# In-projection duals of a hybrid conv block: PSUM pairs that turn, wide additions, q split after DRAM

## The chip, the cores and the metric

The kernel runs on one core of one Trainium2 chip. The metric is the device time of one execution in microseconds; before the change it is 1518.36 us (median of three runs, 1518.31 to 1518.46). A core has TensorE (PE, matmuls into PSUM), VectorE (DVE), ScalarE (ACT), GpSimd (POOL) and SyncE (SP, which here only issues DMAs). PSUM has eight banks of 128 partitions by 512 fp32 words.

## What is computed

One trunk layer on x of 1024 tokens by 1024 channels, float32:

```python
h = rms_norm(x, norm_mix_g) * (1 + sc1) + sh1
b_s, c_s, v_s, v_c, gl_c, gate_br = split(h @ w_in)      # 7 blocks of 1024 columns
y_a = (b_s * causal_dwconv3(c_s * v_s)) @ w_short_out    # the factor before w_short_out is "q"
u   = causal_dwconv31(v_c * sigmoid(gl_c)) + conv_conf_b
y_b = silu(layer_norm(u)) @ w_conf_out
g_a, g_b = split(sigmoid(gate_br))
x = x + g1 * ((g_a * y_a + g_b * y_b) @ w_o)
h2 = rms_norm(x, norm_ffn_g) * (1 + sc2) + sh2
a, b = split(h2 @ w_ffn_in)
x = x + g2 * ((silu(a) * b) @ w_ffn_out)
out = rms_norm(x, final_norm_g)
```

## The kernel before, in words

Activations lie transposed: channels on partitions, tokens along the free dimension, in two halves of 512. Each float32 operand is split into a high and a low part (`th`/`tl` for activations, `wh`/`wl` for weights) and each product is three matmuls (`mm3`, L285, L286, L288). `split_w` makes `wh` on ACT (L207) and `wl` on DVE or, in the in-projection, on POOL (L208).

Most of the in-projection runs in twelve **duals**. A dual works on a pair of entries of `PAIRS`, which are four column blocks of 128, two for each half-index p, as 2 by 2 block matrices multiplied with seven products instead of eight. `PRODUCTS = "1265734"` is their order. The weight sums (`dual_units`, L230 to L234) and the low halves are POOL's. Each product is 2 (p) x 4 (k) x 3 matmuls of 128x512, 24 in all, accumulated in one of three banks per p: x takes products 1, 6, 7 and 4 on top of each other, y takes 2, z takes 5 and 3. A weight set is prepared two products ahead (`AHEAD`), and the plan of weights is fetched by `next_w`.

After each half product, `evac` in `win_evac` (L569) takes the bank's state out: products 1 and 6 are copied by ACT to SBUF (L579), 5 too (L594); 2, 3 and 7 are added by DVE to what lies there (`plus`, L547); 4 goes to its use from PSUM. From these come the four blocks C11, C12, C21, C22 of each entry. Four kinds of entry follow: "u" (the conv's input, v times sigmoid of gl), "p" (c times v, then the 3-tap `short_conv`, L538 and L540, into `sc`), "q" (b times `sc`, L551 and L589), "g" (sigmoid, then a store of the gate to DRAM by ACT's queue, L616). `q_store` (L527) splits q into high and low in a `qs` tile, ACT cast (L531) and POOL subtraction (L532), and stores both by SP (L534). `q_load` (L621) brings the split halves back to operand tiles of the `t` pool by SP, four after each product of the last dual.

Beside the duals DVE runs the 31-tap conv, `conv(j)` for eight channel blocks: 46 taps each (L649) on two PSUM banks of `ps2`, with ACT at its beginning (L653) and end (L662); `add_conv` sums the result on POOL (L669). A tap's place in DVE's order is bounded by `tc.issue_after`: tap n of block j comes after a certain one of the `plus` instructions, listed in `reads`, so that all are spread over the first 66 of the 72. Otherwise the order on each engine is set by a planner that goes by program order as priority and by its own estimate of times; on the chip each engine then runs its instructions in that order. Tiles come from pools with a fixed number of buffers: `uc` (8 of 128x1054) for u, p, sc, sig, qs and cv; `gs` (6 of 128x512) for small results; `ps` (6 single PSUM banks) and `ps2` (2).

After the duals comes `ya`: for each of eight column blocks, q (all eight channel blocks) times `w_short_out`, then the layer norm, `yb`, `mix`, and the FFN.

Of the kernel before, what the change touches and what calls it, by code (L numbers as in the profile page):

```python
# [34 lines left out]
F32 = mybir.dt.float32  # L35
# [4 lines left out]
P = 128  # L40
# [43 lines left out]
CONV_READS = 66  # L84

# [24 lines left out]
def block_kernel(ctx: ExitStack, tc: tile.TileContext, x0, xT, c, vecs, ada, w_first, w_plain, w_duals,  # L110
# [21 lines left out]
    psp = pool("ps", 6, space=bass.MemoryType.PSUM)  # L132
    ps2p = pool("ps2", 2, space=bass.MemoryType.PSUM)
    dram = pool("scratch", 1, space=bass.MemoryType.DRAM)
    gsp = pool("gs", 6)
# [3 lines left out]

    def ps_tile(name):  # L140
        return psp.tile([P, H], F32, tag="ps", name=name)
# [10 lines left out]
    def g_tile(name):  # L152
        return gsp.tile([P, H], F32, tag="gs", name=name)
# [373 lines left out]
    def q_store(j):  # L527

        for h in range(2):
            s = uc_tile("qs", T, F32R)  # L530
            nc.scalar.copy(s[:, :H], sc[j][:, halves[h]])  # L531
            nc.gpsimd.tensor_tensor(s[:, H:], sc[j][:, halves[h]], f32(s[:, :H]), ALU.subtract)  # L532
# [3 lines left out]
    def short_conv(j, p):  # L536
        sc[j] = uc_tile(f"sc{j}", T)
        nc.scalar.activation(sc[j], p[:, :T], AF.Copy, scale=col(V_SW, j))  # L538
        for s in range(1, SK):
            nc.vector.scalar_tensor_tensor(  # L540
                out=sc[j], in0=p[:, s : s + T], scalar=col(V_SW + s * KC, j), in1=sc[j], op0=ALU.mult, op1=ALU.add
            )
# [3 lines left out]
    def plus(out, ps, b):  # L546
        reads.append(nc.vector.tensor_tensor(out, ps, b, ALU.add).ins)  # L547

    def minus_times(out, a, b):

        nc.vector.scalar_tensor_tensor(out=out, in0=a, scalar=-1.0, in1=b, op0=ALU.mult, op1=ALU.mult)  # L551

    def win_evac(pairs):

        st = [{} for _ in pairs]

        def start(e, kind, j):
            if kind == "u":
                u.append(u_tile(j))
                e["b"] = [u[j][:, CK - 1 + h * H : CK - 1 + (h + 1) * H] for h in range(2)]  # L560
            elif kind == "p":
                e["p"] = uc_tile(f"p{j}", T + SK - 1)
                nc.vector.memset(e["p"][:, : SK - 1], 0.0)
                e["b"] = [e["p"][:, SK - 1 + h * H : SK - 1 + (h + 1) * H] for h in range(2)]
            elif kind == "g":
# [3 lines left out]
        def evac(i, m, ps):  # L569
            kind, j, *rest = pairs[i]  # L570
            e = st[i]
            if m == "1":
                start(e, kind, j)
                if kind == "q":
                    e["b"] = [g_tile("m")]
            if m == "6" and kind == "q":
                e["b"].append(g_tile("v"))
            if m in "16":
                nc.scalar.copy(e["b"][m == "6"], ps)  # L579
            elif m in "23":  # L580
                h = m == "3"
                b = e["b"][h]
                plus(b, ps, b)
                if kind == "u" and h:
                    nc.vector.tensor_tensor(b, b, e["z"], ALU.mult)
                elif kind == "p" and h:
                    minus_times(b, e["z"], b)
                elif kind == "q":
                    nc.vector.tensor_tensor(sc[j][:, halves[h]], b, sc[j][:, halves[h]], ALU.mult)  # L589
                elif kind == "g":  # L590
                    nc.scalar.activation(b, b, AF.Sigmoid)
            elif m == "5":
                e["z"] = e["c"][1] if kind == "g" else g_tile("z")
                nc.scalar.copy(e["z"], ps)  # L594
            elif m == "7":
                plus(e["z"], ps, e["z"])
                if kind in "ug":
                    nc.scalar.activation(e["z"], e["z"], AF.Sigmoid, scale=-1.0)
                elif kind == "q":
                    minus_times(sc[j + 1][:, halves[1]], e["z"], sc[j + 1][:, halves[1]])  # L600
            else:
                if kind in "ug":
                    sig = e["c"][0] if kind == "g" else g_tile("sig")
                    nc.scalar.activation(sig, ps, AF.Sigmoid, scale=-1.0)
                if kind == "u":
                    nc.vector.tensor_tensor(e["b"][0], e["b"][0], sig, ALU.mult)
                elif kind == "p":
                    minus_times(e["b"][0], ps, e["b"][0])
                    short_conv(j, e["p"])
                elif kind == "q":  # L610
                    minus_times(sc[j + 1][:, halves[0]], ps, sc[j + 1][:, halves[0]])
                    for i in range(2):
                        q_store(j + i)
                else:
                    for g, t in zip((j, *rest), e["t"]):
                        nc.scalar.dma_start(gate_dram[g], t)  # L616
        return evac
# [15 lines left out]

    def conv(j):
# [4 lines left out]
        with tc.issue_after(reads[j * CONV_READS // KC]):  # L639
            nc.vector.tensor_tensor(d, ev, od, ALU.subtract)  # L640
            nc.vector.tensor_tensor(e, ev[:, 1:], od[:, : NE - 1], ALU.subtract)
# [3 lines left out]
        def tap(out, src, s, wt, acc):  # L645
            nonlocal n
            n += 1
            with tc.issue_after(reads[(j * TAPS + n) * CONV_READS // (KC * TAPS)]):
                tap.ins = nc.vector.scalar_tensor_tensor(  # L649
                    out=out, in0=src[:, s : s + H], scalar=wt, in1=acc, op0=ALU.mult, op1=ALU.add  # L650
                ).ins
# [13 lines left out]
    def add_conv(j):  # L665

        with tc.issue_after(pool_los[(j + 1) * CONV_READS * 7 // (6 * KC) + 5]):
            for h in range(2):
                nc.gpsimd.tensor_tensor(tot[h], tot[h], u[j][:, halves[h]], ALU.add)  # L669
# [65 lines left out]
    for j in range(KC):  # L735
        conv(j)
        add_conv(j)
    ma = {}
# [447 lines left out]
```

## Time and profile before

| what | us |
|---|---|
| median of the runs | 1518.36 |
| span of the profiled execution, first to last instruction | 1514.3 |
| first matmul of the first dual, start | 113.84 |
| end of the twelve duals | 585.04 |
| stage of the duals | 471.20 |
| PE busy in it | 462.30 |
| DVE busy in it | 412.44 |
| POOL busy in it | 376.87 |
| ACT busy in it | 177.94 |

The page gives no time of its own for the profiled execution beside its span; the median of the runs is 4.06 us above that span, and those 4.06 us lie around the first and the last instruction. A line of a group reads: code line, engine, operation, tile written and tiles read, shape, count, then busy time and mean ns of one, then the engine's idle time ahead of it and who ended it. A line of waits reads: who waited, for whom, us in total, times, the longest.

### The profile page before, as it was taken

The numbers are of one execution on the slowest core, as the hardware profiler recorded it, in microseconds if no ns is written. First come the engines' busy times: TensorE is split into PE (matmuls) and PEld (weight loads), VectorE is DVE, ScalarE is ACT, GpSimd is POOL, SyncE is SP. The second block draws the span as 40 slices with busy tenths as digits, with TensorE's granted clock in tenths as the row PEclk, the third lists the DMA queues.
The fourth block names the chain that finished last, engine by engine and source line by source line (L and its number), as shares of the span: only waits on it lengthen the run. The fifth ranks groups of instructions, "written<-read, shape, count | busy, mean of one in ns | idle before, by whom it ended". The sixth has DMA issues, their size and how long they took to land.

```text
span 1514.3 us, 17807 instructions
## 1 busy us (share of the span) xinstructions
PE 1475.4 (97%) x6455; PEld 1203.2 (79%) x6455; DVE 1173.1 (77%) x1561; ACT 613.6 (41%) x875; POOL 580.2 (38%) x483
## 2 busy tenths in 40 slices
PE   6999999999998999999999989999999999999997
PEld 2788887877886888888788868888888888888887
DVE  7897898989998882857876798876666665767755
ACT  4654333333332442325335464444444443211235
POOL 0037788788768884320121101110000006444105
PEclk9999999999999999999999999999999999999999
DMA  9522224223222259655754527644444449997403
GB/s 347 206 64 84 84 71 139 70 98 111 98 84 85 69 192 408 239 197 173 249 193 155 167 89 231 209 153 153 153 153 153 153 150 363 348 330 241 152 28 112
DMA packets 87306, 255.64 MB, mean 169 GB/s; under 512 B 10033, under 2 KB 12209, under 8 KB 87218
## 3 DMA queue, kind: packets, MB, share of 16 engines
q1 hardware_dynamic: 46384, 146.30, 28.9%
q0 software_dynamic: 36944, 95.44, 19.0%
q10 hardware_dynamic: 3890, 12.78, 2.1%
q8 instruction: 50, 0.82, 0.2%
q14 instruction: 38, 0.31, 0.1%
HBM read 187.89 MB, written 66.58 MB: 168 GB/s over the span
## 4 chain that ended last, share of the span: by engine, by line
PE 78%; DVE 10%; POOL 7%; issue 3%; DMA 1%; ACT 1%; SPq 0%; POOLq 0%; ACTq 0%; DVEq 0%
PE x L288 10%; PE x L286 10%; PE x L285 10%; PE z L286 5%; PE z L285 5%; PE z L288 5%; DVE c L649 4%; PE y L288 3%; PE y L285 3%; PE y L286 3%; POOL wl L208 3%; PE ya L285 2%; PE mix L285 2%; PE mix L286 2%; PE ya L288 2%
## 5 line engine op out<-in xcount | busy, mean ns | idle before, releaser
L207 ACT CAST wh<-raw 128x1024 fp32r<-128x1024 f32 (+2 forms) x257 | 259.1, 1009 | 417.0 <-PE x L286 107.0
L208 POOL TENSOR_TENSOR wl<-raw,wh 128x1024 fp32r<-128x1024 f32 x92 | 237.0, 2584 | 87.6 <-ACT wh L207 81.1
L208 DVE TENSOR_TENSOR wl<-raw,wh 128x1024 fp32r<-128x1024 f32 (+2 forms) x165 | 188.1, 1141 | 50.8 <-ACT wh L207 48.4
L649 DVE SCALAR_TENSOR_TENSOR c<-diff,vec,c 128x512 f32<-128x512 f32 x248 | 182.2, 749 | 6.4 <-DMA q<-qs 2.6
L912 POOL DMA_DIRECT2D hid<-stage x71 | 37.9, 534 | 356.7 <-DVE stage L325 351.5
L285 PE MATMUL x<-th,wh 128*128 128x512 f32 x336 | 130.7, 389 | 0.0
L286 PE MATMUL x<-tl,wh 128*128 128x512 f32 x336 | 130.7, 389 | 0.0
L288 PE MATMUL x<-th,wl 128*128 128x512 f32 x336 | 130.7, 389 | 0.0
L649 DVE SCALAR_TENSOR_TENSOR c<-u,wsum,c 128x512 f32<-128x512 f32 x112 | 84.0, 750 | 2.0
L285 PE MATMUL x<-t2h,wh 128*128 128x512 f32 x184 | 73.6, 402 | 5.5 <-ACT wh L207 2.8
L288 PE MATMUL x<-t2h,wl 128*128 128x512 f32 x184 | 73.5, 400 | 4.5 <-POOL wl L208 4.2
L266 DVE CUSTOM_DVE_ANT_0 raw<-raw,cs,vec 128x1024 f32<-128x1024 f32 x24 | 36.9, 1541 | 48.9 <-DMA raw<-in_ada 39.7
L286 PE MATMUL x<-t2l,wh 128*128 128x512 f32 x184 | 73.4, 399 | 0.1
L286 PEld LDWEIGHTS x<-tl,wh 128*128 128x128 f32 x336 | 63.1, 188 | 13.2
L288 PEld LDWEIGHTS x<-th,wl 128*128 128x128 f32 x336 | 63.1, 188 | 13.1
L285 PEld LDWEIGHTS x<-th,wh 128*128 128x128 f32 x336 | 63.1, 188 | 13.0
L230 POOL TENSOR_TENSOR raw<-raw 128x1024 f32<-128x1024 f32 x12 | 29.2, 2437 | 99.1 <-DVE wl L208 95.3
L288 PE MATMUL z<-th,wl 128*128 128x512 f32 x168 | 65.5, 390 | 0.0
L285 PE MATMUL z<-th,wh 128*128 128x512 f32 x168 | 65.4, 389 | 0.0
L286 PE MATMUL z<-tl,wh 128*128 128x512 f32 x168 | 65.4, 389 | 0.0
L324 ACT CAST stage<-g 128x512 fp32r<-128x512 f32 x62 | 38.3, 621 | 54.6 <-DMA hid<-stage 26.8
L325 DVE TENSOR_TENSOR stage<-g,stage 128x512 fp32r<-128x512 f32 x62 | 42.4, 687 | 20.1 <-ACT stage L324 19.9
(802 smaller groups left out, 4076.5 us busy)
## 6 DMA issues: line engine op xcount, KB each, us to landing
hid<-stage POOLq DMA_DIRECT2D x71, 512.0 KB, 4.0
raw<-in_w_fi SPq DMA_DIRECT2D x50, 512.0 KB, 4.4
raw<-in_w_duals SPq DMA_DIRECT2D x48, 512.0 KB, 3.5
th<-hid POOLq DMA_DIRECT2D x71, 256.0 KB, 5.7
tl<-hid POOLq DMA_DIRECT2D x71, 256.0 KB, 5.8
ada<-in_ada SPq DMA_DIRECT2D x24, 512.0 KB, 6.4
raw<-in_ada SPq DMA_DIRECT2D x24, 512.0 KB, 4.5
raw<-in_w_fo SPq DMA_DIRECT2D x24, 384.0 KB, 5.8
```

The lines of the kernel that those rows point to most:

```text
L207: nc.scalar.copy(wh, raw)
L208: lo = lo_engine.tensor_tensor(wl, raw, f32(wh), ALU.subtract)
L230: eng.tensor_tensor(a["s1"], a["21"], a["22"], ALU.add)
L266: nc.vector.tensor_tensor_reduce(out=raw, in0=raw, in1=cs, scale=1.0, scalar=col(V_ADA, b), op0=ALU.mult, op1=ALU.add, accum_out=modc(b),)
L285: nc.tensor.matmul(ps, wh, xh, start=first, stop=False, skip_group_check=again)
L286: nc.tensor.matmul(ps, wh, xl, start=False, stop=False, skip_group_check=again)
L288: mm3.ins = nc.tensor.matmul(ps, wl, xh, start=False, stop=last, skip_group_check=again).ins
L324: nc.scalar.copy(hi, src)
L325: nc.vector.tensor_tensor(lo, src, f32(hi), ALU.subtract)
L649: tap.ins = nc.vector.scalar_tensor_tensor(out=out, in0=src[:, s : s + H], scalar=wt, in1=acc, op0=ALU.mult, op1=ALU.add).ins
L912: nc.gpsimd.dma_start(hid_dram[key], s)
```

## The change

The seven products, their matmuls, the weights' sums and splits, and everything after `ya` stay. In the duals:

- The six single banks are replaced by three pairs `w0`, `w1`, `w2` (each 128x2x512, one bank for each p), which take the roles x, y, z in turn: the next dual's x is this dual's y, its y this z, its z this x.
- After each half of product 1, ACT copies the bank of x into that of y, and product 2 accumulates on that copy (no clearing), so C11 is whole in y.
- Products 6 and 5 are copied by one ACT instruction for both p (`wide`, 128x1024); products 7 and 3 are completed by one wide DVE addition each, whose result is in PSUM (for duals with a q entry, y takes that of product 7; otherwise the SBUF tile).
- The entries' last steps (`c11`, `c22`, `c12`, `c21`) read PSUM, once both p are done. `short_conv` keeps its running sum in the bank pair of x.
- q is stored whole (`sc` itself, one DMA of 512 KB for each j) and loaded whole into a `uc` tile after the last dual's code, then split there by ACT and DVE.
- A tap of the conv is bound to the last read (products 7, 3 and 4 at times 5, 6 and 7 of a dual) that is not later than the tap's own time, which spreads all taps over 11.2 duals. `add_conv` follows.
- In `PAIRS`, ("u", 7) comes before ("p", 6).
- The pools `ps` and `gs` are closed before the duals and opened again after the convs; meanwhile `psw` (the three pairs) and `gsw` (3 tiles of 128x2x512) take their place.

```diff
-    ("q", 4), ("p", 6), ("p", 7), ("u", 7), ("q", 6), ("g", ("a", 2), ("a", 3)),
+    ("q", 4), ("u", 7), ("p", 6), ("p", 7), ("q", 6), ("g", ("a", 2), ("a", 3)),
...
-CONV_READS = 66
+CONV_DUALS = 11.2
+AT_READS = {"7": 5, "3": 6, "4": 7}
...
     def q_store(j):
-        for h in range(2):
-            s = uc_tile("qs", T, F32R)
-            nc.scalar.copy(s[:, :H], sc[j][:, halves[h]])
-            nc.gpsimd.tensor_tensor(s[:, H:], sc[j][:, halves[h]], f32(s[:, :H]), ALU.subtract)
-            q_dram[j, h] = dram.tile([P, T], F32, name=f"q{j}{h}")
-            nc.sync.dma_start(q_dram[j, h], f32(s))
+        q_dram[j] = dram.tile([P, T], F32, name=f"q{j}")
+        nc.sync.dma_start(q_dram[j], sc[j])
...
+    def short_conv(j, p, bank):
         sc[j] = uc_tile(f"sc{j}", T)
-        nc.scalar.activation(sc[j], p[:, :T], AF.Copy, scale=col(V_SW, j))
+        bank = bank.rearrange("p two n -> p (two n)")
+        nc.scalar.activation(bank, p[:, :T], AF.Copy, scale=col(V_SW, j))
         for s in range(1, SK):
             nc.vector.scalar_tensor_tensor(
-                out=sc[j], in0=p[:, s : s + T], scalar=col(V_SW + s * KC, j), in1=sc[j], op0=ALU.mult, op1=ALU.add
+                out=sc[j] if s == SK - 1 else bank, in0=p[:, s : s + T], scalar=col(V_SW + s * KC, j), in1=bank,
+                op0=ALU.mult, op1=ALU.add
             )
...
+        def c11(e, kind, j, *more):
+            if kind == "q":
+                times(sc[j][:, halves[0]], y[:, e["p"]], sc[j][:, halves[0]])
+                return
...
+            nc.scalar.activation(e["b"][0], y[:, e["p"]], AF.Sigmoid if kind == "g" else AF.Copy)
+        def c22(e, kind, j, *more):
+            src = (y if mul else rest["z"])[:, e["p"]]
+            if kind == "q":
+                return minus_times(sc[j + 1][:, halves[1]], src, sc[j + 1][:, halves[1]])
+            if kind == "p":
+                e["z"] = src
+            else:
+                e["z"] = e["c"][1] if kind == "g" else rest["z"][:, e["p"]]
+                nc.scalar.activation(e["z"], src, AF.Sigmoid, scale=-1.0)
+        def c12(e, kind, j, *more):
+            src = z[:, e["p"]]
...
+            if kind == "u":
+                return times(e["b"][1], src, e["z"])
+            if kind == "p":
+                return minus_times(e["b"][1], src, e["z"])
+            nc.scalar.activation(e["b"][1], src, AF.Sigmoid)
+        def c21(e, kind, j, *more):
+            src = x[:, e["p"]]
...
+            if kind == "u":
+                nc.scalar.activation(src, src, AF.Sigmoid, scale=-1.0)
+                return times(e["b"][0], src, e["b"][0])
+            nc.scalar.activation(e["c"][0], src, AF.Sigmoid, scale=-1.0)
...
+        banks = {"1": x, "6": x, "7": x, "4": x, "2": y, "5": z, "3": z}
+        for m in PRODUCTS:
+            w = next_w()
+            for p in both:
+                ps = banks[m][:, p]
+                for k in range(KH):
+                    c0 = (p * KH + k) * P
+                    mm3([ps], slice(c0, c0 + P), w, [th[m][k]], m in "15" and k == 0, k == KH - 1, m not in "15")
+                if m == "1":
+                    nc.scalar.copy(y[:, p], ps)
+            if m == "2":
+                finals(c11, m)
+            elif m in "65":
+                rest[m] = rest["z"] = wide("v")
+                nc.scalar.copy(rest[m], x if m == "6" else z)
             elif m == "7":
+                add = nc.vector.tensor_tensor(y if mul else rest["5"], x, rest["5"], ALU.add)
+                finals(c22, m, add.ins)
+            elif m == "3":
+                add = nc.vector.tensor_tensor(z, z, rest["6"], ALU.add)
+                finals(c12, m, add.ins)
+            elif m == "4":
+                finals(c21, m)
...
-    def q_load(j, h):
-        qT[j][h] = t_pair(f"q{j}{h}")
-        for t, s in zip(qT[j][h], halves):
-            nc.sync.dma_start(f32(t), q_dram[j, h][:, s])
+    def q_load(j):
+        t = uc_tile("q", T)
+        nc.sync.dma_start(t, q_dram[j])
+        for h in range(2):
+            qT[j][h] = split(t[:, halves[h]], hl_tile, f"q{j}{h}")
...
+    def paced(n):
+        at = 7 * CONV_DUALS * n / (KC * TAPS)
+        return [ins for when, ins in reads if when <= max(at, reads[0][0])][-1]
...
+    close(*small)
+    small = open_pool("psw", 1, space=bass.MemoryType.PSUM), open_pool("gsw", 3, side="right")
+    banks = [small[0][1].tile([P, 2, H], F32, tag=f"w{i}", name=f"w{i}") for i in range(3)]
     for d in range(n_duals):
-        banks, evac = {}, win_evac(PAIRS[2 * d : 2 * d + 2])
-        for i, m in enumerate(PRODUCTS):
-            product(banks, m, th[m], evac, y_tile=ps_tile)
-            if d == n_duals - 1:
-                for n in range(4 * i, min(4 * i + 4, 2 * KC)):
-                    q_load(n // 2, n % 2)
+        win_dual(d, PAIRS[2 * d : 2 * d + 2], *banks)
+        banks.append(banks.pop(0))
+    for j in range(KC):
+        q_load(j)
...
+    close(*small)
+    small = singles(ctx)
```

More of the change, by code (lines that the diff above doesn't have):

```diff
@@ L561, in start @@
             elif kind == "p":
[L562 to L565, printed above, removed]
+                e["t"] = uc_tile(f"p{j}", T + SK - 1)
+                nc.vector.memset(e["t"][:, : SK - 1], 0.0)
+                e["b"] = [e["t"][:, SK - 1 + h * H : SK - 1 + (h + 1) * H] for h in range(2)]
+            else:
@@ L566, in start @@
                 e["t"] = [uc_tile("sig", T) for _ in range(2)]
                 e["b"], e["c"] = ([t[:, s] for s in halves] for t in e["t"])
[L569 to L594, printed above, removed]
-            elif m == "7":
[L596 to L616, printed above, removed]
```

54 lines of the change are left out of this document (40 added, 14 removed).

## The prediction

> **What bounds the kernel now.** I read the page first, then the twelve duals of the in-projection one by one, then who waited for whom in them, then the engines' lines there. The page:
>
> ```profile
> PE 1475.4 (97%) x6455; PEld 1203.2 (79%) x6455; DVE 1173.1 (77%) x1561; ACT 613.6 (41%) x875; POOL 580.2 (38%) x483
> ```
>
> TensorE (PE) is the bound, and the change leaves its matmuls alone: only time in which PE waits can be won. A dual begins with its first matmul on h00h (24 such, two halves in each of twelve duals); the windows below run from one such start to the next (columns: busy time and count of PE, PEld, DVE, ACT, POOL; granted clock; DMA share; GB/s).
>
> ```profile
> L285 PE MATMUL x<-h00h,wh x24: 389/389/389, 113.8 to 549.7; 128*128 128x512 f32 x24
> ```
>
> ```profile
> 113.84:151.92 38.08, 38.08 (x169) 31.53 (x168) 29.46 (x39) 15.55 (x21) 28.39 (x15) 1.00 0.25 83
> ...
> 228.08:267.34 39.26, 38.88 (x170) 31.30 (x168) 33.70 (x53) 14.56 (x20) 33.70 (x18) 1.00 0.39 134
> ...
> 305.42:345.60 40.18, 38.71 (x170) 31.38 (x168) 36.41 (x44) 15.45 (x21) 36.23 (x16) 1.00 0.28 95
> 345.60:385.46 39.86, 38.41 (x169) 31.46 (x168) 37.96 (x55) 15.82 (x22) 34.88 (x17) 1.00 0.31 106
> ...
> 461.62:508.88 47.26, 41.66 (x169) 33.60 (x168) 37.90 (x54) 15.78 (x20) 40.61 (x18) 0.93 0.26 89
> 508.88:546.96 38.08, 38.08 (x169) 31.53 (x168) 37.33 (x43) 13.12 (x19) 33.39 (x17) 1.00 0.27 83
> 546.96:585.04 38.08, 38.08 (x169) 31.53 (x168) 17.44 (x25) 16.22 (x24) 25.09 (x13) 1.00 0.88 330
> sum 471.20, PE 462.30 PEld 379.99 DVE 412.44 ACT 177.94 POOL 376.87; mean PE 38.53 PEld 31.67 DVE 34.37 ACT 14.83 POOL 31.41
> ```
>
> A dual without a stall takes 38.08 us, that is 5.44 a product and 2.72 a half of one. Twelve would take 456.96; they take 471.20. The loss is 14.24 us, in four duals: 1.18, 2.10, 1.78 and 9.18. The last one holds two stalls and a lower clock behind them (0.93). DVE is busy 412.44 of 471.20, 88%. Who waited, in this stage:
>
> ```profile
> POOL wl L208 <- ACT wh L207: 62.7, 22, 5.9
> ACT u L662 <- DVE c L649: 44.4, 12, 6.8
> ACT sig L591 <- DVE sig L547: 35.3, 11, 6.6
> ...
> ACT qs L531 <- DVE sc L589: 18.7, 5, 7.0
> ACT sc L538 <- DVE p L551: 18.6, 7, 5.7
> ACT qs L531 <- DVE sc L551: 12.6, 4, 7.0
> ...
> PEld x L288 <- POOL wl L208: 9.4, 5, 3.3
> ...
> PE x L288 <- POOL wl L208: 7.4, 4, 2.8
> ```
>
> PE waits for the low halves of the weights (wl, POOL), POOL for their high halves (wh, ACT), and ACT stands in its own order behind results of a late DVE. Ahead of the worst stall, ACT and then POOL:
>
> ```profile
> 437.35 0.72 ACT L662 ACTIVATE u<-c,vec 128x512 f32<-128x512 f32 x1 [6.80 <-DVE c L649]
> ...
> 460.01 0.62 ACT L531 CAST qs<-sc 128x512 fp32r<-128x512 f32 x1 [6.98 <-DVE sc L589]
> ```
>
> ```profile
> 440.55 1.31 POOL L532 TENSOR_TENSOR qs<-sc,qs 128x512 fp32r<-128x512 f32 x1 [7.09 <-ACT qs L531]
> ...
> 462.22 2.81 POOL L208 TENSOR_TENSOR wl<-raw,wh 128x1024 fp32r<-128x1024 f32 x1
> ```
>
> POOL lost 7 us at a qs subtraction, and the wl that the dual at 461.62 needs for its first product is made only from 462.22 to 465.03.
>
> **The change part by part.** DVE and POOL rows of the stage, then those of the conv's line:
>
> ```profile
> L540 DVE SCALAR_TENSOR_TENSOR sc<-p,vec,sc 128x1024 f32<-128x1024 f32 x16 | 39.6, 2477 | 1.3 <-ACT sc L538 1.3
> L606 DVE TENSOR_TENSOR u<-u,sig 128x512 f32<-128x512 f32 x5 | 12.7, 2535 | 0.0
> L547 DVE TENSOR_TENSOR z<-x,z 128x512 f32<-128x512 f32 x17 | 11.6, 685 | 18.5 <-PE x L288 18.5
> L551 DVE SCALAR_TENSOR_TENSOR p<-z,p 128x512 f32<-128x512 f32 x8 | 11.4, 1430 | 0.0
> ...
> L551 DVE SCALAR_TENSOR_TENSOR sc<-z,sc 128x512 f32<-128x512 f32 x4 | 6.5, 1626 | 0.0
> ...
> L551 DVE SCALAR_TENSOR_TENSOR p<-x,p 128x512 f32<-128x512 f32 x8 | 5.4, 678 | 0.0
> ```
>
> ```profile
> L532 POOL TENSOR_TENSOR qs<-sc,qs 128x512 fp32r<-128x512 f32 x16 | 23.5, 1480 | 7.1 <-ACT qs L531 7.1
> ```
>
> ```profile
> L540 DVE SCALAR_TENSOR_TENSOR sc<-p,vec,sc x16: 1278/2760/3333, 151.4 to 510.2; 128x1024 f32<-128x1024 f32 x16
> ```
>
> ```profile
> L208 DVE TENSOR_TENSOR wl<-raw,wh 128x1024 fp32r<-128x1024 f32 x110 | 134.0, 1220 | 47.3 <-ACT wh L207 45.0
> ```
>
> Wide additions and M2 in PSUM: six half additions a dual go (72 at 0.685, 49.3 us), two wide ones come. A 1024-wide one costs between 1.22 (row of wl) and two halves, 1.37; I take 1.22, the same shape, so 24 cost 29.3: 20.0 saved. Operands in PSUM: lines whose inputs all lie in SBUF take two to four times what the same shapes take with one in PSUM (1430 against 678 on L551). Short conv: at its own fastest, 1.28, 16 cost 20.5 instead of 39.6, 19.1 saved. L606 at 0.68: 3.4 instead of 12.7, 9.3 saved. L551 p<-z, sc<-z: 6.0 and 3.8 saved. Together 58 us: DVE falls from 412 to about 354 of 457, 77%. If PSUM operands brought nothing beside POOL, it would be the 20.0 alone, 392, 86%. I take 354: the cheap rows lie in the same stretches as the dear ones.
>
> q whole: 16 casts on ACT and 16 subtractions on POOL (23.5) leave the duals: POOL falls from 376.9 to 353.4 of 457.0, 77%, and stands at no qs any more (7.1). The store waits on SP's queue for DVE alone; behind it stand weight loads, which are two products ahead, so nothing for that.
>
> M2 on a copy of M1: ACT writes M1 into the next bank pair, half by half, and M2's half waits for it. This wait is new.
>
> ```profile
> L579 ACT COPY p<-x 128x512 f32<-128x512 f32 x16 | 9.3, 582 | 9.4 <-PE x L288 8.5 <-ACT sig L604 0.5 <-ACT sig L430 0.4
> ...
> L653 ACT ACTIVATE c<-u,wsum 128x512 f32<-128x512 f32 x7 | 5.1, 724 | 4.1 <-DVE u L606 3.9
> ```
>
> The copy costs 0.58 (from PSUM) to 0.72 (into PSUM). Its time is 2.72 us, the other half's matmuls. Where ACT is free (dual at 423.54) today's copy of the second half starts 6.43 us into the dual; M2's second half starts at 8.16: 1.1 us to spare. The latest one in the trace:
>
> ```profile
> 429.97 0.58 ACT L579 COPY p<-x 128x512 f32<-128x512 f32 x1
> ```
>
> ```profile
> 514.10 0.39 PE L288 MATMUL x<-h30h,wl 128*128 128x512 f32 x1
> ...
> 517.04 0.39 PE L285 MATMUL y<-h40h,wh 128*128 128x512 f32 x1
> ```
>
> ```profile
> 517.94 0.57 ACT L579 COPY sig<-x 128x512 f32<-128x512 f32 x1
> ```
>
> It ends at 518.51, 1.5 us after 517.04. So 0 to 1.5 a dual, 0 to 18 us in all. I take 2.1 (0.7 in three duals): that lateness is DVE's, which gets 58 us back.
>
> Three pairs in turn: the next M1 goes where y was, not where x was; a pair's results have 5.44 us or more before it is written again, against 2.72 today. The row shows no wait there today: 0. ACT's extra copies of p and u out of PSUM (13 at 0.58, 7.6) and the narrower count of wide ones balance against 178 of 471: 0. Taps by time: their number stays; they may run from M7 of the first dual instead of M2, and the last are released by the end of the eleventh dual, 38 us ahead of the stage's end, where the weights of conv (L662) wait least: 0. The PAIRS order only moves u7 ahead of p6: 0.
>
> The end of the stage: q is loaded whole (8 loads on SP instead of 32 of half the size) into uc buffers and split there, 16 casts on ACT and 16 subtractions on DVE.
>
> ```profile
> DMA to landing us min/median/max: 4.0/5.1/7.8
> ```
>
> ```profile
> L325 DVE TENSOR_TENSOR tl<-x,th 128x512 fp32r<-128x512 f32 x4 | 6.9, 1784 | 0.0
> ```
>
> The subtractions cost 0.68 to 1.78 each, 11 to 29 us; DVE is busy only 17.4 of 38.08 in the last dual (row above), and the operand buffers come free product by product there, as they do for today's loads. Cover: that dual and the 9.5 us until the first ya product needs its last q. I take 0; without the cover see below.
>
> Sum: 14.24 - 2.1 = 12.1 us less. Against the profiled execution, whose span is 1514.3, the span becomes 1502.2; the median of the runs, 1518.36, lies 4.1 above that span and I move it along: **1506.3**. Less than 0.2% (3 us) is about what a measurement of this kernel cannot tell from no change.
>
> **The rivals.** *M2 waits for ACT in every dual (slower).* ACT is in order, and the copy can stand behind a wait for DVE: 5.7 (L538) or 6.8 us (L662) at the longest. For it: L538 follows M4, just ahead of M1. Against it: L538 waited 7 times and 18.6 us in all, 2.7 at a mean, on a DVE at 88%. At the latest copy's 1.5 in all twelve it costs 18, and 14.24 comes back: 1522. It decides from 14.24/12 = 1.2 a dual. At 6.8 each, 6.8 + 0.58 - 2.72 = 4.7 in twelve, 56: 1560, the far end. The clock row (0.93 over 47.26, 3.3 us lost behind two stalls of about 3) says long waits cost more than themselves, some 1.7 each. The Trainium skill, "TensorE: Matmul & The Clock Gate", Part 1, says that an idle window of about 3.4 us halves the clock; this trace agrees with about that size (0.93), and by it the far end would be some 20 us further, while waits of 1.5 cost only themselves.
>
> *q is late for ya (slower).* The uc buffers also hold four sig tiles and u7 in the last dual. With one free, q after q: 5.1 (today's median landing) + 0.62 + 0.62 + 1.78 = 8.1 (casts as L531), eight 65 us from M2's end (10.9 into the dual), 76, against 47.6 allowed: 28 lost, 1518.4 - 12.1 + 28 = 1534. With two free it halves to 43 and is hidden. For it: buffers; against: q0 to q5 are stored long before. The Trainium skill, "GPSIMD Engine Reference", 1. Specifications, says that VectorE shares its SBUF interfaces with GpSimd and that instructions with two SBUF inputs contend; the rows of L551 above agree, and by it these subtractions take the dear end, 29 us instead of 11.
>
> *POOL stays late.* wl and the weight sums are untouched, 353 of 457 us; if ACT's waits for the conv's end (44.4) remain, half or more of the stalls may stay: 1511 to 1518.
>
> **How the numbers follow.** Forecast 0.58 (its own range 1503 to 1510), POOL stays late 0.14, M2 waits 0.18, q late 0.10. Faster by over 0.2% (below 1515.3): 0.58 + 0.07 + 0.02 = 0.67; within it 0.08; slower 0.25. Low end 1502: all 14.24 and 2 us more where a clock drop elsewhere falls otherwise. High end 1521: nearly the whole of the near price of M2's waits; beyond it lie about 0.15.
>
> **What would show it.** Right: twelve duals near 38.1 each with clock 1.00; no qs lines; the short conv at about 1.28; DVE near 354 in the stage; waits of POOL for wh and of PE for wl nearly gone; ya's first product 457 us or so after the first M1. Wrong: PE waiting on y for an ACT copy, or on z or x for a wide one; a gap ahead of the first ya; duals still stalled on wl.

## The result and the profile after

The changed kernel takes 1571.91 us (median; 1569.93 to 1574.46) against 1518.34 for the kernel before on the same chip: 1.036 times as long, 95% interval 1.0347 to 1.0377. It is slower by 3.6%, where 1506.3 was forecast. The profiled execution has a span of 1569.0 us against 1514.3, that is 54.7 more. (The 4.06 us that the text ahead of the prediction puts between the median and the span do not all lie around the first and the last instruction: the changed kernel's profiled execution took 1570.78 us with a span of 1569.0, 1.8 apart, and the other runs are alike. The rest of the 4.06, some 2 us, is then a difference between two executions, and the forecast is too high by so much and no more.) The head of its page:

```profile
span 1569.0 us, 17634 instructions
PE 1492.1 (95%) x6455; PEld 1208.8 (77%) x6455; DVE 1141.8 (73%) x1529; ACT 618.3 (39%) x864; POOL 535.2 (34%) x467
```

DVE, POOL and the count of instructions all fell, as the change wanted; PE has the same 6455 matmuls, is busy 16.7 us longer for them, and the share fell from 97% to 95%. The next view cuts the span at each dual's first matmul on h00h, as in the prediction (columns: window and its length; busy time and count of PE, PEld, DVE, ACT, POOL; granted clock; DMA share; GB/s).

```profile
116.03:156.44 40.41, 38.84 (x169) 31.41 (x169) 11.80 (x12) 11.23 (x14) 25.54 (x12) 1.00 0.20 65
156.44:202.38 45.94, 41.19 (x170) 32.92 (x168) 42.31 (x57) 15.92 (x20) 27.20 (x13) 0.93 0.24 80
...
373.98:414.30 40.32, 38.70 (x169) 31.30 (x168) 29.46 (x41) 14.28 (x18) 28.83 (x14) 1.00 0.23 79
...
589.07:633.24 44.17, 39.19 (x170) 31.04 (x168) 13.86 (x18) 16.14 (x23) 22.34 (x12) 1.00 0.59 194
sum 517.21, PE 475.76 PEld 383.23 DVE 373.84 ACT 173.64 POOL 331.41; mean PE 39.65 PEld 31.94 DVE 31.15 ACT 14.47 POOL 27.62
```

Not one dual takes 38.08 any more. Six take 40.3 to 40.8, five take 45.0 to 47.0, and the last takes 44.17 with the wait of ya at its end. The stage is 517.21 instead of 471.20 (46.0 more), it starts 2.2 later (116.03 against 113.84), and what follows it is 6.5 longer (935.78 against 929.26, from the first ya matmul to the end): 46.0 + 2.2 + 6.5 = 54.7. Against twelve undisturbed duals (456.96) the stage loses 60.25: PE is idle for 517.21 - 475.76 = 41.45, and busy 475.76 - 456.96 = 18.80 longer for the same matmuls, most of it at the lower clock of 0.93 to 0.96.

Who waited for whom in the stage (total, times, longest):

```profile
POOL wl L213 <- ACT wh L212: 178.6, 52, 9.7
...
PEld w L290 <- ACT w L628: 34.7, 23, 4.5
PE w L290 <- ACT w L628: 26.8, 14, 4.1
...
PE w L290 <- ACT wh L212: 8.1, 9, 1.0
...
PE w L290 <- ACT sig L435: 3.2, 1, 3.2
PE w L290 <- DVE u L423: 3.1, 1, 3.1
```

L628 is the new copy of M1 into the next pair. It runs 24 times, and 23 weight loads of PE wait for it. No wait of PE for wl, the stalls of before, is left: POOL waits nearly three times as long for wh as it did (178.6 against 62.7 us) and delays nobody by it. The groups by line:

```profile
L290 PE MATMUL w<-h00h,wh 128*128 128x512 f32 x24 | 11.6, 485 | 26.5 <-ACT w L628 23.3 <-ACT sig L435 3.2
...
L290 PE MATMUL w<-h40h,wh 128*128 128x512 f32 x24 | 10.0, 418 | 3.5 <-ACT w L628 3.5
```

They put 23.3 of the 26.8 us ahead of matmuls on h00h and only 3.5 ahead of h40h. That is not where the forecast looked: h40h begins M2, but h00h begins M1 itself. PE in a dual with nothing else wrong (start, duration, operation, and idle time before it):

```profile
376.48 0.39 PE L293 MATMUL w<-h30h,wl 128*128 128x512 f32 x1
377.52 0.50 PE L290 MATMUL w<-h00h,wh 128*128 128x512 f32 x1 [0.66 <-ACT w L628]
...
380.16 0.39 PE L293 MATMUL w<-h30h,wl 128*128 128x512 f32 x1
381.51 0.50 PE L290 MATMUL w<-th,wh 128*128 128x512 f32 x1 [0.96 <-ACT wh L212]
```

And ACT in the same stretch:

```profile
376.90 0.57 ACT L628 COPY w<-w 128x512 f32<-128x512 f32 x1 [1.35 <-PE w L293]
380.41 1.04 ACT L212 CAST wh<-raw 128x1024 fp32r<-128x1024 f32 x1 [2.94 <-PE w L291]
381.36 0.58 ACT L628 COPY w<-w 128x512 f32<-128x512 f32 x1
```

A half of a product is 12 matmuls in 2.72 us, 0.227 apart, so M1's second half was due at 376.71. It starts at 377.52, right behind the copy of the first half (376.90 + 0.57). The two halves write different banks, yet the second waits until the first bank has been read. Then the copy of the second half waits for that half to end and stands behind a cast of weights (380.41 to 381.45); it ends at 381.94. PE's order in ten of the twelve duals has two matmuls of product 5 ahead of M2, and the weights that this cast makes are theirs: they start at 381.51, and M2 follows at 382.08, behind the copy. The two delays, 0.81 and 1.12 (381.51 against 380.39), with slower starts behind each, are the 2.24 us that this dual has over 38.08. A bad dual, PE and then ACT:

```profile
204.87 0.39 PE L293 MATMUL w<-h30h,wl 128*128 128x512 f32 x1
209.04 0.50 PE L290 MATMUL w<-h00h,wh 128*128 128x512 f32 x1 [3.78 <-ACT w L628]
...
209.86 0.63 PE L290 MATMUL w<-h10h,wh 128*128 128x512 f32 x1
210.29 0.63 PE L291 MATMUL w<-h10l,wh 128*128 128x512 f32 x1
```

```profile
206.06 0.58 ACT L607 ACTIVATE w<-w 128x512 f32<-128x512 f32 x1 [2.59 <-DVE p L552]
207.39 1.12 ACT L541 ACTIVATE w<-p,vec 128x1024 f32<-128x1024 f32 x1 [0.76 <-DVE u L555]
208.45 0.54 ACT L628 COPY w<-w 128x512 f32<-128x512 f32 x1
```

Here the copy was due at 205.1, when M1's first half was done, but ACT stands in its own order behind L607 and the short conv's first multiply, both of the dual before and both waiting for DVE. PE idles 3.78 us, and then its matmuls start 0.43 apart instead of 0.227.

The end of the stage, the 20 us from the first ya matmul on, after and before:

```profile
633.24:653.24 20.00, 18.80 (x57) 13.00 (x58) 13.09 (x18) 11.45 (x19) 4.24 (x2) 0.75 1.02 413
```

```profile
585.04:605.04 20.00, 20.00 (x86) 15.88 (x85) 5.77 (x6) 5.97 (x8) 8.23 (x5) 1.00 1.02 415
```

PE does 57 matmuls where it did 86, at a clock of 0.75. SP's queue says why:

```profile
623.53 0.38 SPq L198 DMA_DIRECT2D raw<-in_ada  x1
623.96 1.92 SPq L657 DMA_DIRECT2D q<-q  x4
628.85 0.33 SPq L198 DMA_DIRECT2D raw<-in_w_short  x1
634.81 0.32 SPq L657 DMA_DIRECT2D q<-q  x1
```

Before, the first q load left 26.9 us ahead of the first ya matmul (558.1 against 585.04). Now the eight loads stand behind weight loads that wait for their own buffers, and four of them wait besides, 12.6 us in all, for stores of the gates out of uc tiles, until 634.81 and later.

### The profile page after: what moved, and what is told of

It reads as the page before. It is cut to its first block, busy times and chain, and to the rows that moved or that the text cites. A ratio compares the mean times of both kernels' runs of the same rounds, so it can differ in the third digit from the quotient of the medians.

```text
span 1569.0 us, 17634 instructions
## 1 busy us (share of the span) xinstructions
PE 1492.1 (95%) x6455; PEld 1208.8 (77%) x6455; DVE 1141.8 (73%) x1529; ACT 618.3 (39%) x864; POOL 535.2 (34%) x467
## 4 chain that ended last, share of the span: by engine, by line
PE 85%; DVE 8%; ACT 2%; DMA 2%; issue 2%; POOL 0%; SPq 0%; POOLq 0%; ACTq 0%; DVEq 0%
PE w L290 8%; PE w L291 8%; PE w L293 8%; PE x L293 7%; PE x L291 7%; PE x L290 7%; PE z L290 3%; PE z L291 3%; PE z L293 3%; PE y L291 3%; PE y L290 3%; PE y L293 3%; DVE c L689 2%; PE ya L291 2%; PE ya L293 2%; PE ya L290 2%
## 5 line engine op out<-in xcount | busy, mean ns | idle before, releaser
L290 PE MATMUL w<-th,wh 128*128 128x512 f32 x288 | 113.5, 394 | 11.4 <-ACT wh L212 8.1
L291 PE MATMUL w<-tl,wh 128*128 128x512 f32 x288 | 112.3, 390 | 0.0
L293 PE MATMUL w<-th,wl 128*128 128x512 f32 x288 | 112.0, 389 | 0.0
L271 DVE CUSTOM_DVE_ANT_0 raw<-raw,cs,vec 128x1024 f32<-128x1024 f32 x24 | 32.4, 1354 | 59.0 <-DMA raw<-in_ada 59.0
L290 PEld LDWEIGHTS w<-th,wh 128*128 128x128 f32 x288 | 54.1, 188 | 27.2 <-ACT wh L212 12.3
L293 PEld LDWEIGHTS w<-th,wl 128*128 128x128 f32 x288 | 54.1, 188 | 11.2
L291 PEld LDWEIGHTS w<-tl,wh 128*128 128x128 f32 x288 | 54.2, 188 | 10.8
L290 PE MATMUL x<-th,wh 128*128 128x512 f32 x144 | 56.0, 389 | 0.0
L291 PE MATMUL x<-tl,wh 128*128 128x512 f32 x144 | 56.0, 389 | 0.0
L293 PE MATMUL x<-th,wl 128*128 128x512 f32 x144 | 56.0, 389 | 0.0
L290 PE MATMUL yb<-zsh,wh 128*128 128x512 f32 x128 | 50.0, 391 | 3.3 <-DVE gb L818 3.3
```

The costliest lines, as they stand in the source:

```text
L271: nc.vector.tensor_tensor_reduce(out=raw, in0=raw, in1=cs, scale=1.0, scalar=col(V_ADA, b), op0=ALU.mult, op1=ALU.add, accum_out=modc(b),)
L290: nc.tensor.matmul(ps, wh, xh, start=first, stop=False, skip_group_check=again)
L291: nc.tensor.matmul(ps, wh, xl, start=False, stop=False, skip_group_check=again)
L293: mm3.ins = nc.tensor.matmul(ps, wl, xh, start=False, stop=last, skip_group_check=again).ins
```

## The experiments

Two theories of the waits in the duals. Theory A: the pair is one tile, so its two banks are ordered as one; M1's second half waits for the copy of the first half, and M2 for the copy of the second, in every dual. Theory B: the copies are late because ACT stands behind a late DVE, whatever the tiles are. Every kernel below computes the same outputs. "Stage" is from the first M1 matmul to the first ya matmul, "after-stage" from there to the end. Both are read from one profiled execution of each kernel, and executions of one kernel differ by some us: the third experiment's ten runs go from 1514.21 to 1521.57, and the profiled one is the slowest; the ninth's five go from 1500.13 to 1505.94, and the profiled one is the fastest. The ratios are of all runs, each to the kernel before on the same chip (the ninth and tenth experiments ran on another chip than the first eight).

**First: single-bank tiles.** The three pairs become six tiles; the wide copies, additions and the short conv go by halves.

```diff
-    banks = [small[0][1].tile([P, 2, H], F32, tag=f"w{i}", name=f"w{i}") for i in range(3)]
+    banks = [[small[0][1].tile([P, H], F32, tag=f"w{i}{p}", name=f"w{i}") for p in range(2)] for i in range(3)]
...
-                    nc.scalar.copy(y[:, p], ps)
+                    nc.scalar.copy(y[p], ps)
```

> The three pairs become six single banks, each a tile of its own; the wide copies, the wide additions and the short conv are done in halves, all else is as after the change. Theory A (the pair is one tile: the second half of product 1 waits for ACT's copy of the first half, and product 2 for the copy of the second): both waits lose their cause, the duals go from 517 us to 458 to 470, the run from 1572 to 1513 to 1525. Theory B (the copies are late because ACT stands behind a late DVE, whatever the tiles): the 4 us waits stay, only moved from product 1 to product 2; duals 495 to 510, the run 1550 to 1565.

Measured: 1519.63 us, 1.0024 times the kernel before (1.0015 to 1.0034); the span is 50.2 us shorter than the changed kernel's. The longest of its duals, and the sum of all:

```profile
191.31:231.41 40.10, 38.39 (x169) 31.46 (x168) 39.03 (x58) 14.49 (x20) 29.64 (x14) 1.00 0.28 90
...
sum 460.91, PE 458.15 PEld 378.07 DVE 371.65 ACT 182.13 POOL 335.99; mean PE 38.18 PEld 31.51 DVE 30.97 ACT 15.18 POOL 28.00
```

Eight duals of twelve take 38.08, and the stage falls from 517.21 to 460.91 with the same copies on the same busy ACT. The edit also makes the other wide instructions narrow, which the time alone does not tell apart from the tiles; the rows do. In a dual of this kernel, PE and then ACT:

```profile
310.06 0.39 PE L293 MATMUL w<-h30h,wl 128*128 128x512 f32 x1
310.29 0.39 PE L290 MATMUL w<-h00h,wh 128*128 128x512 f32 x1
```

```profile
310.49 0.57 ACT L628 COPY w<-w 128x512 f32<-128x512 f32 x1 [0.62 <-PE w L293]
```

M1's second half starts 0.23 us behind the last matmul of the first, before the copy has begun, and M2 follows with no matmul of product 5 ahead of it. The programs say the same: in the changed kernel the first matmul of M1's second half has to wait for the copy of the first in each of the duals, and with single banks it has not. Theory A holds. What B explains is the rest, waits for the copy of 2.3 us in all. The after-stage grew to 943.99, though, with waits of the ya products for q30h, q40h, q41l and q50h, 3.7 us the longest.

**Second: one copy for both halves,** behind the whole of M1, in the pairs as they are.

```diff
-                if m == "1":
-                    nc.scalar.copy(y[:, p], ps)
+            if m == "1":
+                nc.scalar.copy(y, x)
```

> Only this: product 1 is copied by one wide ACT instruction after both halves. Theory A: product 1's second half waits no more, product 2 waits in every dual for one wide copy and the cast of a weight ahead of it, about 2 us; duals near 481 to 490, the run 1536 to 1545. Theory B: the late copies are as late as before, duals 500 to 515, the run 1555 to 1570.

Measured: 1545.05 us, 1.0188 (1.0172 to 1.0203); stage 492.91, quiet duals 39.5 to 40. M1's second half no longer waits for a copy. Between M1 and M2, PE now waits in every dual: for the copy of 1.0 us (8.7 us in ten waits), for the cast of the weights of the two matmuls of product 5 (5.6 in six), and in two duals for DVE (4.4 and 1.3). That is 24 us less stage than with the copy by halves: in a pair the copy by halves makes PE wait twice, and the first of these waits, behind ACT's leftovers of the dual before, is the long one.

**Third: M2 starts its own bank,** with no copy into PSUM; M1 is copied wide into SBUF, and a third wide addition per dual joins them on DVE.

```diff
-                    mm3([ps], slice(c0, c0 + P), w, [th[m][k]], m in "15" and k == 0, k == KH - 1, m not in "15")
-                if m == "1":
-                    nc.scalar.copy(y[:, p], ps)
+                    mm3([ps], slice(c0, c0 + P), w, [th[m][k]], m in "125" and k == 0, k == KH - 1, m not in "125")
+            if m == "1":
+                rest["1"] = wide("v")
+                nc.scalar.copy(rest["1"], x)
             if m == "2":
+                nc.vector.tensor_tensor(y, y, rest["1"], ALU.add)
                 finals(c11, m)
```

> Product 2 accumulates in its pair alone; product 1 goes by one wide copy to SBUF and DVE adds it in a third wide addition a dual. Nothing on PE waits for an ACT copy between products 1 and 2. Theories A and B both: duals 457 to 465; the start of the duals and of ya still as late as after the change (8 to 9 us together): the run 1512 to 1524. If it stays above 1540, something else than the copy holds PE.

Measured: 1518.67 us, 1.0015 (1.0002 to 1.0027). All duals but the first and the last take 38.08, with pairs and at 382.8 us of DVE:

```profile
116.89:158.00 41.11, 41.11 (x169) 33.74 (x170) 13.05 (x13) 11.20 (x13) 25.52 (x12) 0.92 0.20 64
...
538.79:581.54 42.75, 38.54 (x169) 31.27 (x167) 18.03 (x21) 16.16 (x22) 22.36 (x12) 0.99 0.62 218
sum 464.65, PE 460.44 PEld 380.35 DVE 382.83 ACT 173.79 POOL 332.81; mean PE 38.37 PEld 31.70 DVE 31.90 ACT 14.48 POOL 27.73
```

So the pairs cost nothing by themselves inside the duals; the copy from one PSUM pair to another, which M2 needs at once, does. The first dual is left with a start that waited 3.2 us for the sigmoid of L435 and ran at the lower clock behind it, the last with the wait of ya for q. After-stage 938.26.

**Fourth: the kernel before with q whole alone.**

```diff
-        for h in range(2):
-            s = uc_tile("qs", T, F32R)
-            nc.scalar.copy(s[:, :H], sc[j][:, halves[h]])
-            nc.gpsimd.tensor_tensor(s[:, H:], sc[j][:, halves[h]], f32(s[:, :H]), ALU.subtract)
-            q_dram[j, h] = dram.tile([P, T], F32, name=f"q{j}{h}")
-            nc.sync.dma_start(q_dram[j, h], f32(s))
+        q_dram[j] = dram.tile([P, T], F32, name=f"q{j}")
+        nc.sync.dma_start(q_dram[j], sc[j])
...
```

> The kernel before with one part of the change alone: q stored whole, loaded whole after the duals and split there by ACT and DVE. By the trace of after, ya starts 3 to 6 us late for q, and POOL and ACT lose the qs work in the duals, where up to 9 of 14 us of stalls hung on it: the run 1511 to 1526. If q is the larger part of the loss, 1540 or more.

Measured: 1514.53 us, 0.9985 (0.9975 to 0.9994), a gain at the edge of what can be told. It is two larger effects against each other: the stage falls by 9.0 to 462.20, with one stalled dual instead of four, now that ACT and POOL have no qs work in the duals; the after-stage grows by 5.6 to 934.84, with waits of PE for q31l and q61l of 2.1 and 2.2 us.

**Fifth: the first one with the old way of q** (split by ACT and POOL, stored and loaded in halves, loads in the last dual). Theory Q1: q whole is what delays ya. Theory Q2: ya is late for the banks that are closed and opened again behind the stage.

> The changed kernel with single-bank tiles (as the first experiment), and with the old way of q: split by ScalarE and GpSimd, stored and loaded in halves, the loads in the last dual. Theory Q1 (q whole is what delays the ya products): after-stage back from 944.0 to 929 to 931 us, the stage 461 to 465 (GpSimd has its 16 subtractions, 23 us, again), span 1504 to 1510. Theory Q2 (the ya products are late for another cause, the banks that close and open again behind the stage): after-stage stays 938 to 944, span 1514 to 1522.

Measured: 1517.57 us, 1.0007 (0.9997 to 1.0016); stage 465.87, with one dual of 43.07 in which PE waits 3.3 us for a late copy; after-stage 937.53. The after-stage lies between the two forecasts. Of the 14.7 us by which the first experiment's is longer than that of the kernel before (943.99 against 929.26), the old way of q takes back 6.5. Q1 is not the whole of it: the 32 q loads are issued from 28.5 to 5.8 us ahead of the first ya matmul, and ya waits 5.3 us all the same, for a sigmoid.

**Sixth: the third one with single banks and the old way of q.**

> As the run above, but product 2 starts its own bank, and a third addition per dual on VectorE takes the place of the copy into PSUM (as the third experiment, with single-bank tiles). Q1: stage 457 to 461, since in the third experiment ten duals of twelve took 38.08 and the other two are accounted for by the pair tile at the start and by q at the end; after-stage 929 to 931; span 1500 to 1506, the fastest. Rival: the third addition (24 x 0.7 us, some 16 us of VectorE) and GpSimd's q work bring the stalls on wl back: stage 465 to 471, span 1508 to 1515. Q2: 1511 to 1517.

Measured: 1508.98 us, 0.9955 (0.9944 to 0.9967): the first version of the new duals that is faster than the kernel before. Stage 458.08: the feared return of the wl stalls did not come, at 380 us of DVE and 354 of POOL. After-stage 935.73, and its rows show Q2 at work. PE, then ACT:

```profile
571.71 0.39 PE L291 MATMUL ya<-q00l,wh 128*128 128x512 f32 x1
576.88 0.80 PE L290 MATMUL ya<-q01h,wh 128*128 128x512 f32 x1 [4.79 <-ACT sig L613]
```

```profile
573.29 1.04 ACT L212 CAST wh<-raw 128x1024 fp32r<-128x1024 f32 x1 [8.44 <-DMA gate_a<-sig]
...
576.24 0.60 ACT L613 ACTIVATE sig<-w 128x512 f32<-128x512 f32 x1 [0.40 <-ACT sig L613]
```

The second half of the first ya product starts when the last sigmoid of product 4 has read its bank. That sigmoid stands on ACT behind a weight cast that waits 8.44 us for a transfer, with the 16 DMA engines full (share 1.03). The row names a gate's store; the weight load itself was issued at 565.61 and landed at 573.19, 0.1 us ahead of the cast. The kernel before has the same wait on ACT there, 8.90 us, and loses nothing by it: as the programs are allocated, its first two ya tiles have the banks of product 2 of the last dual, while here the second of them has bank 7, that of product 4's second half.

**Seventh: the changed kernel with the old way of q alone.**

> The changed kernel as it is, pairs as one tile, with the old way of q alone. Q1: the stage stays near 517 (515 to 523, the waits for the copies are untouched), after-stage 929 to 931 instead of 935.8, span 1561 to 1569. Q2: after-stage near 936, span 1567 to 1575. If the waits in the duals came from q's share of ScalarE's order, the stage would fall below 510.

Measured: 1563.23 us, 1.031 (1.0295 to 1.0324); stage 515.28, after-stage 930.08. So q whole is 5.7 us of the after-stage's 6.5, and the waits in the duals have nothing to do with it. Q1 holds in this kernel, as far as 0.7 us, which PE waits for the sigmoid: its stage ends 61 us later than in the sixth, and the cast ahead of the sigmoid is done in time.

**Eighth: the first one with q whole, its loads and splits placed inside the last dual** instead of behind all duals.

```diff
+            if d == n_duals - 1 and i >= 3:
+                for n in range(2 * i - 6, 2 * i - 4):
+                    q_load(n)
```

> Single-bank tiles and q whole, but the eight loads and splits stand in the program inside the last dual, two behind each of products 5, 7, 3 and 4, instead of behind all duals. If the loads' place on SP's queue behind weight loads is what makes q late: first loads some 10 to 30 us ahead of the ya products instead of at their start, after-stage 929 to 935, span 1504 to 1512. If it is the buffers they share with the gates, or the splits' 11 to 29 us on VectorE: after-stage 938 to 944 as in the first experiment, span 1514 to 1522.

Measured: 1510.41 us, 0.9964 (0.9953 to 0.9976); stage 460.94, after-stage 934.25. The after-stage and the span are as the first of the two expectations has them: of the first one's 944.0, 9.7 us were the place of the loads and splits in the program, behind weight loads on SP's queue; waits of 2.4 for the sigmoid and 2.0 for q51l are left.

**Ninth: the sixth with the three pairs begun one place further on,** so that product 4 of the last dual uses banks 4 and 5.

```diff
+    banks = banks[2:] + banks[:2]
     for d in range(n_duals):
```

> The sixth experiment with the three bank pairs begun one place further on, so that the last dual's product 4 does not use the bank that the second half of the first ya product is given (the ya product then takes a bank of product 2, read 25 us earlier). If the wait of 4.8 us for the gate's last sigmoid is a wait for that bank: gone, no lower clock behind it, after-stage 929 to 931 instead of 935.7, stage 458, span 1500 to 1503. If ya is late for data (q's halves, or its weight behind the same full DMA engines): after-stage stays 933 to 936, span 1505 to 1508.

Measured: 1503.74 us, 0.9911 (0.9895 to 0.9927), 0.9% faster than the kernel before. PE waits for nobody in the whole stage:

```profile
sum 456.95, PE 456.95 PEld 378.50 DVE 379.62 ACT 186.29 POOL 354.29; mean PE 38.08 PEld 31.54 DVE 31.64 ACT 15.52 POOL 29.52
```

and the 20 us behind it are full again:

```profile
570.68:590.68 20.00, 20.00 (x86) 15.88 (x85) 3.79 (x6) 5.93 (x8) 9.79 (x6) 1.00 1.03 419
```

After-stage 927.67, a little under the expectation, in the fastest of five runs. One line moved the ratio from 0.9955 to 0.9911, which is 6.7 us, and the span of the profiled executions from 1507.2 to 1498.4, which is 8.8. ACT's weight cast waits here too, 7.73 us, and PE does not: the wait was one for a bank. The first dual, 38.87 in the sixth, takes 38.08 with the same line.

**Tenth: the ninth with q whole, loaded early.**

> As the run above, but q whole, with its loads and splits placed inside the last dual (as in the eighth). ScalarE and GpSimd lose their 16 casts and 16 subtractions in the duals, VectorE gets 16 subtractions in the last one. If q whole is free once its loads are early and the bank is another: span 1499 to 1503, as above or up to 1 us faster. If the splits still come late for some ya products (q51l kept ya 2.0 us in the eighth): after-stage 932 to 934, span 1503 to 1506, slower than the run above.

Measured: 1507.73 us, 0.9941 (0.9927 to 0.9954); stage 456.96 again, after-stage 934.14, with waits for q50h, q51h, q50l and q51l (2.0 the longest) and a clock of 0.91 over its first 20 us. With no stalls left in the duals, q whole has nothing to give there and costs time at ya: 6.5 us between the two profiled executions, 4.0 between the medians (1507.73 against 1503.74, same chip).

## Why the prediction was wrong

**The step that failed is "M2 on a copy of M1".** It priced the copy half by half, with the other half's 2.72 us of matmuls as cover, and came to 0 to 1.5 us a dual, 2.1 in all. In the changed kernel there is no other half to run beside the copy: the two banks of a pair are one tile, so M1's second half waits for the copy of the first (23.3 us of PE's idle time), and M2 for the copy of the second and the cast ahead of it. The least is 2.24 us in a dual, and the mean over the twelve is 60.25 / 12 = 5.0, the last one's wait for q included. The step's arithmetic would have held for single-bank tiles: the first experiment has waits for the copy of 2.3 us in all, against the forecast 2.1. That the two are so near is in part luck: in the fifth, with the same copies, they are 5.4. What was missing is one question at the line that makes the banks: what unit does a wait see? The tile's shape, two halves in one, stood in the diff.

**The second error is its lateness.** The forecast took DVE's relief to make ACT punctual. ACT's order did not change: the dual's last results (L607, L609, L541) come ahead of the copy, and each waits for DVE's last instructions on the same dual. In the kernel before, the next matmul into the bank that is copied was product 6's, three halves (8.16 us) after that half of M1 was done; here M1's second half needs the copy at once. The latest copy seen before, 1.5 us late, was no bound for that.

**"The end of the stage: 0" failed too.** The term named two covers, the last dual and 9.5 us until the last q is needed. The seventh experiment puts it at 5.7 us; the tenth, where the loads start early, still has 4.0 to 6.5. The loads did not start in the last dual, since on SP's queue they stand behind weight loads that wait for buffers; the step had counted the loads, but not what is queued ahead of them.

**"Three pairs in turn: 0" was wrong in one dual and at both edges of the stage.** The term counted 5.44 us or more from a pair's last results to its next product, by the order of the products. PE's order takes two matmuls of product 5 ahead of M2, and they go into the pair in which the short conv of the dual before keeps its sum. In the dual at 414.30 that sum is late, PE and then DVE:

```profile
425.74 0.77 PE L290 MATMUL w<-th,wh 128*128 128x512 f32 x1 [3.07 <-DVE u L423]
```

```profile
424.32 1.27 DVE L543 SCALAR_TENSOR_TENSOR sc<-p,vec,w 128x1024 f32<-128x1024 f32 x1
```

The copy of M1 was done at 424.01, so 1.7 of the 3.1 us are the pair's. (The row names L423, a short instruction that DVE ran next; the last read of the pair is L543's, and it ends at 425.59.) The first M1 starts 2.2 us later, since its tile covers a bank that a gate's sigmoid (L435) still reads; with single banks the stage starts at 113.91. At the other end the reopened banks cost 0.7 us in the seventh and some 7 to 8 in the sixth (after-stage 935.73 against 927.67 in the ninth, 6.7 by the ratios).

**What was right.** The 14.24 us of stalls were there to be had, and all came back in the ninth kernel (456.95). The prices of operands in PSUM held:

```profile
L680 DVE TENSOR_TENSOR diff<-u 128x527 f32<-128x527 f32 x8 | 16.9, 2113 | 0.1
L681 DVE TENSOR_TENSOR diff<-u 128x526 f32<-128x526 f32 x8 | 15.9, 1991 | 0.0
L638 DVE TENSOR_TENSOR w<-w,v 128x1024 f32<-128x1024 f32 x12 | 14.7, 1227 | 1.4 <-PE w L293 1.3
L543 DVE SCALAR_TENSOR_TENSOR w<-p,vec,w 128x1024 f32<-128x1024 f32 x8 | 10.3, 1284 | 2.9 <-ACT w L541 2.9
L543 DVE SCALAR_TENSOR_TENSOR sc<-p,vec,w 128x1024 f32<-128x1024 f32 x8 | 10.2, 1274 | 0.0
...
L635 DVE TENSOR_TENSOR v<-w,v 128x1024 f32<-128x1024 f32 x8 | 9.8, 1223 | 78.8 <-PE w L293 78.8
...
L271 DVE CUSTOM_DVE_ANT_0 raw<-raw,cs,vec 128x1024 f32<-128x1024 f32 x3 | 5.6, 1856 | 26.7 <-DMA raw<-in_ada 26.7
...
L635 DVE TENSOR_TENSOR w<-w,v 128x1024 f32<-128x1024 f32 x4 | 4.9, 1232 | 17.1 <-PE w L293 17.1
...
L555 DVE TENSOR_TENSOR u<-w,u 128x512 f32<-128x512 f32 x5 | 3.5, 692 | 0.2
```

The wide additions cost 14.7 + 9.8 + 4.9 = 29.4 (29.3 forecast), the short conv 20.5 (20.5), the line that was L606 3.5 (3.4). DVE came to 373.84 and not 354: the differences of the conv, whose inputs still lie in SBUF, went from 1333 and 1174 ns to 2113 and 1991, 12.7 us in all, and 5.6 us of modulation work (L271) fell into the stage. The forecast had taken the dear rows as removed, and the price as one of SBUF operands alone (two to four times), though the kernel before has L589 with both inputs in SBUF at 755 to 773 ns; part of the price turned up again at the next lines of the kind. It did not matter: the ninth kernel has 379.6 us of DVE and no stall.

**The rivals.** "M2 waits for ACT in every dual" had the right engine and sign. Its far end, 1560, came near for another reason: it took 6.8 us of lateness in every dual and a cover of 2.72, where PE idled over 3 us at a stretch in five duals and had no cover. That it came within 12 us is luck. Its allowance of some 1.7 us for the clock behind a long wait was of the right kind: the 18.80 us of longer busy time are mostly that. The Trainium skill, "TensorE: Matmul & The Clock Gate", Part 1, gives the idle window as about 3.4 us. The traces agree with that in size only. In the changed kernel no gap of up to 2.6 us between matmuls of the stage was followed by a spacing of 0.43, and six of the seven gaps of 3.2 to 4.2 us were (the one ahead of the first ya matmul among them), for 6 to 15 matmuls; the seventh, of 3.4 us ahead of the first M1, was not. But a wait of 2.84 us was followed by it in the kernel before (at 465.08), and one of 1.88 us in the second experiment (at 292.47), for 8 matmuls. "q is late for ya" was true, in its place and its cause (uc buffers among them), at a fifth of its 28 us. "POOL stays late" is out: no PE wait for wl is left in any of the duals after the change.

## What to carry to other kernels

Before a wait is priced, ask what the unit is that it sees: a tile of two banks is released and claimed as one, and a half-by-half pipeline over it is none; six tiles in place of three, with the wide instructions cut to fit, gave 50 us back. A value that is needed within microseconds must not be made on an engine that works in order and stands behind another engine's results; the addition at the end (third and ninth experiments) costs that other engine 15 to 17 us and the kernel nothing. When stalls go, look at what the earlier end of the stage runs into: here a queue (q's loads) and a bank. The bank is not a matter of time alone: ACT's last sigmoid was as late in the kernel before, and cost nothing there because the next product had been given other banks.

## What was not expected of the hardware

- Full DMA engines at the end of the stage (share 1.02 to 1.03, 413 to 419 GB/s) go with a wait of ACT's next weight cast of 7.7 to 8.9 us, in the kernel before too. The load that this cast waits for took 7.6 us from issue to landing in the sixth experiment, and the weight load ahead of the q loads 3.9. It costs time only where a PSUM bank's last reader stands behind that cast on ACT: 4.8 us of idle PE and a clock of 0.91 over the next 20 us in the sixth experiment, none in the ninth, where the cast waits 7.73 us.
- DVE's subtraction of two SBUF operands, 128x527, took 1333 ns at a mean before and 2113 after, with no change of its own. What differs is what POOL does meanwhile. Of the 192 subtractions of this kind (128x527 and 128x526) in the twelve kernels' traces, the 43 during which POOL was idle (busy under 5% of their time) took 0.69 to 0.71 us each. The 113 during which it was busy throughout (95% or more) took 0.68 to 2.92, 2.2 at a mean; why some of these stay at 0.7 is open.
- A copy from PSUM to PSUM on ACT is no dearer than one into SBUF: 536 to 595 ns for 128x512 (L628), against 582 for the copy into SBUF before.
